# A two-layer decoder trunk on one core: a new opening with plain fp32 products, another PSUM bank for the compression, and layer 1's last sums in place

## The chip, the core and the metric

One core of a Trainium2 chip runs the kernel in one launch. Its engines are TensorE (PE, with its weight loads as PEld), VectorE (DVE), ScalarE (ACT), GpSimd (POOL) and SyncE (SP), which issues most of the transfers. The metric is the device time of one execution in microseconds, as the median of several runs; lower is better.

## What is computed

Two layers over a sequence of 1024 tokens and a width of 1024. The core of the reference, cut:

```python
def reference(x, c, positions, w_in, ..., w_up, w_down):
    cond = jax.nn.silu(c)
    for l in range(DEPTH):
        mod = cond @ w_mod[l] + b_mod[l]
        sh1, sc1, gt1, sh2, sc2, gt2 = [m[:, None, :] for m in jnp.split(mod, N_MOD, axis=-1)]
        h = rms_norm(x, norm_g[l, 0]) * (1.0 + sc1) + sh1
        y = mixer_block(h, positions, w_in[l], ..., w_o[l])
        x = x + gt1 * rms_norm(y, norm_g[l, 1])
        h = rms_norm(x, norm_g[l, 2]) * (1.0 + sc2) + sh2
        y = jnp.square(jax.nn.relu(h @ w_up[l])) @ w_down[l]
        x = x + gt2 * rms_norm(y, norm_g[l, 3])
    return x
```

`mixer_block` projects h with one matrix w_in and feeds four groups of 256 features: a gated convolution of width 3, a sparse attention (its keys and values compressed by blocks of 32 tokens with `cmp_w1`, `cmp_w2` and a position table `cmp_pos`, selected blocks, and a window), a gated linear attention, and a chunked gMLP. Each group's output is normalised, and the four go through one output projection w_o.

## The kernel before

Activations lie feature-major, in tiles of 128 features x 512 tokens; the sequence is two halves `hf` of T = 512 tokens, and eight tiles k = 0..7 make the width. A product is taken in three passes over fp32r tiles that are split into a high and a low part (`mm3`, L174 to L177): high by high, high by low, low by high. `gemm` (L179) does this for one output tile over eight k, and fetches the weights in units of four k: a transfer to `raw_a`, `raw_b` or `raw_f`, a cast on ACT (L167) and a subtraction on DVE (L131) give `w_a`, `w_b`, `w_f`. The letter is the lane, with buffers of its own.

The order of the program is `start()`, `mix(0,0)`, `mix(0,1)`, `ff(0,0)`, `mix(1,0)`, `ff(0,1)`, `mix(1,1)`, `ff(1,0)`, `ff(1,1)`, with layer and half as arguments. The order of the instructions on each engine is made from this by the scheduler of the language: an instruction stands the earlier the higher its rank, and `tc.high_priority(offset=-LATER[l, hf])` lowers the rank of a mixer's residual and of the norm behind it. Tiles of a named region may take the space of a region that was closed, tile by tile, as soon as its last reader is done. PSUM has eight banks, by tags: `mm` 2, `ff` 2, `s` 2, `t` 1, `pv` 1.

`start()` (L269) makes the rope tables (17 x 512 products, sent to DRAM as `cosd` and `sind`), the silu of the condition (`cond`, L293 to L296), the norm factor R of the first half (`rms_R`, L192 to L204: squares on ACT, sums on DVE, one product with a matrix of ones), and then for each k: two dots of a 512 KB slab of w_mod with cond (L243), the modulated tile h as a split pair (`make_h`, L207 to L213), and the six `EARLY` column blocks of w_in by `mm3`, from weights `w_k` that were split from `raw_k`: 8 x 6 x 3 = 144 products into six banks.

`mix(0,0)` runs gates, attention (`nsa_part`, with `compress()`, the scores L829 and L831, transposes L784 and weighted sums L789 and L790), and beside it, in lane b, the projections of the other groups (384 products `ps_mm<-h,w_b`), with two half dots per unit for the rest of the modulation (`mods_now`, L251). `compress()` has 32 products of tokens with `cmp_w1` (`ps_mm<-bp,kvt`, L717) and 32 of the position table (`ps_mm<-bp,p`, L717), sums of four partial results (L726, L737) and two small products (L747, L754), all in the `mm` banks. The output projection w_o follows (`ps_mm<-h,w_a`).

`ff_body` goes over eight groups of four hidden tiles: `up` makes hidden tiles by `gemm`, `down` adds a group's 8 x 12 products to the eight sums y. The last group's sums are written to new tiles `yf` of a region "fin", whose space is that of the mixer that ran beside, and `finish` normalises them and adds the residual, with tiles `xo` that come from DRAM. In the last body, `ff(1,1)`, the last group is done in place. The mixer's own residual (L957 to L963) does the same with tiles `yo`, and `make_h` gives h for the up-projection of the same half.

Of the kernel before, what the change touches and what calls it, by code (L numbers as in the profile page):

```python
# [9 lines left out]
I32 = mybir.dt.int32  # L10
# [8 lines left out]
LATER = {(0, 0): 0, (0, 1): 800, (1, 0): 800, (1, 1): 800}  # L19
# [16 lines left out]
def trunk_kernel(ctx, tc, xT, c, pos, freq, sel, w_in, conv_w, cmp_pos, cmp_w1, cmp_w2,  # L36
# [70 lines left out]
    def load_params(l, names):  # L107
        src = {"ng": norm_g, "bmod": b_mod, "conv": conv_w, "gain": gains}
        for n in names:
            dma(out=par[l][n], in_=src[n][l])  # L110
# [95 lines left out]

    def make_h(xt, R, Ac, shc, ks=range(8)):  # L207
        h = []
        for k in ks:
# [59 lines left out]
    def start():  # L269
        d = par[0]  # L270
        early = {}
        rope_tables()
        with region("kw", "right") as kw, region("su") as su:
            def mk(src, shape):
                t = su.tile(shape, F32, name="mw", tag="mw", bufs=4)
                dma(out=t, in_=src)
                return t

            def wload(n, kh):
                raw = kw.tile([128, 4, 128], F32, name="raw_k", tag="raw_k", bufs=6)  # L280
                dma(out=raw, in_=w_in[0, n, :, 4 * kh:4 * kh + 4, :])
                return raw

            def wsplit(raw):
                hi, lo = (kw.tile([128, 4, 128], F32R, name="w_k", tag="w_k", bufs=12) for _ in range(2))
                A.copy(hi, raw)
                sub(lo, raw, hi.bitcast(F32))
                return hi, lo

            for hf in range(2):  # L290
                t1, t2 = (su.tile([128, T], F32, name="ct", tag="ct", bufs=4) for _ in range(2))
                ch = cond[:, hf * T:hf * T + T]
                dma(out=ch, in_=c[:, hf * T:hf * T + T].to_broadcast([128, T]))  # L293
                logsig(t2, ch, t1)
                A.activation(t2, t2, AF.Exp)
                mul(ch, ch, t2)  # L296
            xt = load_x(0)
            load_params(0, ("ng", "bmod"))
            R = rms_R(xt, 1.0 / 1024)
            bm = d["bmod"].rearrange("p (j k) -> p j k", k=8)  # L300
            hs = []
            for k in range(8):
                ma = work.tile([128, 2, 1], F32, name="ma", tag="ma", bufs=4)
                for j in (0, 1):
                    mod_dot(0, j, k, mk, ma[:, j, :])
                add(d["mod"][:, 0:2, k:k + 1], ma, bm[:, 0:2, k:k + 1])
                mod_scale(0, 1, slice(k, k + 1))
                if k % 4 == 0:
                    raws = [wload(n, k // 4) for n in EARLY]
                hs += make_h(xt, R, d["A1"], d["mod"][:, 0, :], (k,))  # L310
                if k % 4 == 0:
                    ws = {n: wsplit(r) for n, r in zip(EARLY, raws)}
                for i, n in enumerate(EARLY):
                    if k == 0:
                        early[n] = ps(("mm", "mm", "ff", "ff", "s", "s")[i])
                    hi, lo = ws[n]
                    mm3(early[n], hi[:, k % 4, :], lo[:, k % 4, :], hs[k][0], hs[k][1], k == 0, k == 7)
        load_params(0, ("conv", "gain"))
        load_params(1, ("ng", "bmod", "conv", "gain"))
# [26 lines left out]
    def rope_tables():  # L346
        with region("rp") as rp:
# [3 lines left out]
            fr = rp.tile([128, 1, 8], F32, name="fr")  # L351
            dma(out=fr, in_=freq.unsqueeze(0).to_broadcast([128, 1, 8]))
            sl = rp.tile([17, 256], F32, name="sl")
            dma(out=sl, in_=sel)
            pi = rp.tile([128, 8, 1], I32, name="pi")
            dma(out=pi, in_=pos.unsqueeze(2))
# [22 lines left out]
            for hf in range(2):  # L379
# [5 lines left out]
                for w, dst in ((0, cosd), (128, sind)):  # L385
                    p = ps("s")
# [243 lines left out]
    def nsa_part(l, hf, h, rg, gates, early={}):  # L630
# [70 lines left out]

        def compress():
# [8 lines left out]
            def partial(col):  # L711

                hid = ps("mm", (128, 2, 128))
# [31 lines left out]
            kc = ps("mm", (128, 2, 64))  # L745
# [6 lines left out]
            vc = ps("mm", (128, 64))  # L752
# [225 lines left out]
    def ff_body(l, hf, step):  # L978
# [88 lines left out]

    h, early = start()
# [96 lines left out]
```

## Time and profile before

| | us |
|---|---|
| median of 3 runs (lowest, highest) | 2611.32 (2610.13, 2612.88) |
| the profiled execution | 2618.0 |
| its span, first to last instruction | 2616.3 |
| PE busy | 2488.0 (95% of the span) |
| DVE busy | 1631.3 (62%) |
| ACT busy | 1308.9 (50%) |
| mean granted clock of PE | 0.980 |

Times in the profile count from the first instruction of the span. A busy PE can run at a clock below its full one, so the windows give the granted clock beside the busy time. A plain product of two fp32 tiles appears as two records of one instruction, so "x2" is one product.

### The profile page before, as it was taken

How to read it: one execution, taken by the hardware profiler on the slowest of the kernel's cores; microseconds unless marked ns; L12 is line 12 of the kernel's file. 1: busy time of each engine (PE TensorE's matmuls, PEld its weight loads, DVE VectorE, ACT ScalarE, POOL GpSimd, SP SyncE). 2: the span in 40 equal slices, each digit the busy share in tenths (PEclk: the TensorE clock that was granted, in tenths of full speed). 3: DMA queues.
4: the chain of work that ended last, by engine and by line, in shares of the span. 5: the costliest groups of instructions: out<-in, count | busy, mean ns of one | idle time of the engine just before them, and what ended most of it. 6: DMA issues, size and time to landing. Idle time of an engine off the chain costs nothing.

```text
span 2616.3 us, 34392 instructions
## 1 busy us (share of the span) xinstructions
PE 2488.0 (95%) x11834; PEld 1985.6 (76%) x11834; DVE 1631.3 (62%) x3425; ACT 1308.9 (50%) x2657; POOL 53.9 (2%) x65
## 2 busy tenths in 40 slices
PE   5798899999999999999999999999999997999997
PEld 3666677777777878887787787877788875788886
DVE  7697675467887587445676476554577745634445
ACT  3465545445565456344365455444466744443433
POOL 0100000010000000000100000000100000000000
PEclk9898899999999999999999999999999999999999
DMA  8443233355434444223423354322422134333332
GB/s 280 141 151 94 91 122 121 110 152 153 127 117 142 153 157 146 93 78 105 146 77 92 94 157 141 103 81 77 121 74 69 61 107 150 127 98 97 97 97 75
DMA packets 176200, 305.79 MB, mean 117 GB/s; under 512 B 21573, under 2 KB 33434, under 8 KB 176026
## 3 DMA queue, kind: packets, MB, share of 16 engines
q1 hardware_dynamic: 176026, 303.60, 37.6%
q8 instruction: 93, 1.52, 0.2%
q14 instruction: 81, 0.66, 0.1%
HBM read 281.50 MB, written 17.83 MB: 114 GB/s over the span
## 4 chain that ended last, share of the span: by engine, by line
PE 83%; DVE 8%; DMA 5%; ACT 2%; issue 1%; SPq 0%; DVEq 0%; ACTq 0%
PE ps_ff L175 17%; PE ps_ff L176 17%; PE ps_ff L177 17%; PE ps_mm L176 7%; PE ps_mm L177 7%; PE ps_mm L175 7%; DMA raw_f<-in_w_mod_dram 2%; PE ps_mm L784 1%; DMA raw_b<-in_w_mod_dram 1%; PE ps_pv L790 1%; PE ps_pv L789 1%; PE ps_s L829 1%; PE ps_t L199 1%; PE ps_s L831 1%; PE ps_t L784 1%
## 5 line engine op out<-in xcount | busy, mean ns | idle before, releaser
L167 ACT CAST w_f<-raw_f 128x512 fp32r<-128x512 f32 x504 | 311.8, 619 | 430.5 <-PE ps_ff L176 409.0
L131 DVE TENSOR_TENSOR w_f<-raw_f,w_f 128x512 fp32r<-128x512 f32 x504 | 350.7, 697 | 177.7 <-ACT w_f L167 166.6
L175 PE MATMUL ps_ff<-hid,w_f 128*128 128x512 f32 x992 | 395.2, 399 | 21.4 <-DVE yf L137 12.7
L177 PE MATMUL ps_ff<-h,w_f 128*128 128x512 f32 x1024 | 405.4, 396 | 1.2 <-DVE w_f L131 1.2
L176 PE MATMUL ps_ff<-h,w_f 128*128 128x512 f32 x1024 | 402.7, 393 | 0.0
L175 PE MATMUL ps_ff<-h,w_f 128*128 128x512 f32 x1024 | 402.7, 393 | 0.0
L176 PE MATMUL ps_ff<-hid,w_f 128*128 128x512 f32 x992 | 392.1, 395 | 1.5 <-DVE hid L131 1.5
L177 PE MATMUL ps_ff<-hid,w_f 128*128 128x512 f32 x992 | 391.3, 394 | 0.0
L175 PE MATMUL ps_mm<-h,w_a 128*128 128x512 f32 x784 | 317.1, 405 | 6.2 <-ACT h L226 5.1
L177 PE MATMUL ps_mm<-h,w_a 128*128 128x512 f32 x784 | 315.7, 404 | 6.7 <-DVE w_a L131 6.7
L176 PE MATMUL ps_mm<-h,w_a 128*128 128x512 f32 x784 | 313.6, 401 | 1.2 <-DVE h L131 1.2
L167 ACT CAST w_a<-raw_a 128x512 fp32r<-128x512 f32 x196 | 121.3, 620 | 297.7 <-PE ps_mm L176 276.8
L131 DVE TENSOR_TENSOR w_a<-raw_a,w_a 128x512 fp32r<-128x512 f32 x196 | 135.0, 690 | 171.2 <-ACT w_a L167 167.3
L175 PEld LDWEIGHTS ps_ff<-hid,w_f 128*128 128x128 f32 x992 | 187.8, 189 | 69.7 <-DVE yf L137 15.2
L177 PEld LDWEIGHTS ps_ff<-h,w_f 128*128 128x128 f32 x1024 | 192.3, 188 | 45.8 <-issue 3.4
L175 PEld LDWEIGHTS ps_ff<-h,w_f 128*128 128x128 f32 x1024 | 192.4, 188 | 42.6 <-issue 3.1
L176 PEld LDWEIGHTS ps_ff<-h,w_f 128*128 128x128 f32 x1024 | 192.4, 188 | 42.0 <-issue 2.2
L176 PEld LDWEIGHTS ps_ff<-hid,w_f 128*128 128x128 f32 x992 | 187.9, 189 | 44.4 <-issue 2.9
L177 PEld LDWEIGHTS ps_ff<-hid,w_f 128*128 128x128 f32 x992 | 187.8, 189 | 41.2 <-issue 1.4
L137 DVE TENSOR_TENSOR y<-y,ps_ff 128x512 f32<-128x512 f32 (+1 forms) x208 | 138.0, 664 | 123.7 <-PE ps_ff L177 122.4
L175 PEld LDWEIGHTS ps_mm<-h,w_a 128*128 128x128 f32 x784 | 149.3, 190 | 45.8 <-ACT h L226 6.7
L177 PEld LDWEIGHTS ps_mm<-h,w_a 128*128 128x128 f32 x784 | 149.0, 190 | 44.9 <-DVE w_a L131 8.6
(390 smaller groups left out, 3618.3 us busy)
## 6 DMA issues: line engine op xcount, KB each, us to landing
raw_f<-in_w_up_dram SPq DMA_DIRECT2D x256, 256.0 KB, 2.7
raw_f<-in_w_down_dram SPq DMA_DIRECT2D x256, 256.0 KB, 2.7
raw_a<-in_w_in_dram SPq DMA_DIRECT2D x132, 256.0 KB, 2.7
raw_f<-in_w_mod_dram SPq DMA_DIRECT2D x112, 256.0 KB, 2.8
raw_a<-in_w_o_dram SPq DMA_DIRECT2D x64, 256.0 KB, 2.7
raw_b<-in_w_mod_dram SPq DMA_DIRECT2D x48, 256.0 KB, 2.9
mw<-in_w_mod_dram SPq DMA_DIRECT2D x16, 512.0 KB, 5.1
bp<-in_cmp_w_dram SPq DMA_DIRECT2D x32, 256.0 KB, 5.3
```

The lines of the kernel that those rows point to most:

```text
L131: V.tensor_tensor(out=out, in0=a, in1=b, op=ALU.subtract)
L137: eng.tensor_tensor(out=out, in0=a, in1=b, op=ALU.add)
L167: A.copy(hi, raw)
L175: PE.matmul(ps_ap, wh, xh, start=start, stop=False)
L176: PE.matmul(ps_ap, wh, xl, start=False, stop=False)
L177: PE.matmul(ps_ap, wl, xh, start=False, stop=stop)
L199: PE.matmul(p, ones, acc, start=True, stop=True)
L784: PE.transpose(tp[0:kn, hh, :], cols(h0 + hh), ident)
L789: PE.matmul(pv[:, h0:h0 + nh, :], vst, th[0:kn], start=first[0], stop=False)
L790: PE.matmul(pv[:, h0:h0 + nh, :], vst, tl[0:kn], start=False, stop=last)
L829: PE.matmul(sp[:, 0:w], qh[:, h0 + hh, :], KX[:, 128 * k0:128 * k0 + w], start=True, stop=False)
L831: PE.matmul(sp[:, 0:w], ql[:, h0 + hh, :], KX[:, 128 * k0:128 * k0 + w], start=False, stop=True)
```

## The change

1. `start()` is written anew. The condition's transfers and the first two slabs of w_mod are issued first, then x, the six first halves of the early weights (`raw_k`, 4 of 8 k), slabs for k = 1 and 2, and the six late halves (`w_r`). The slabs have 6 buffers for 4. The eight squares go to PE one by one, as plain fp32 products with ones that accumulate. For k < 4 each early block has one plain fp32 product, raw weights by the unsplit tile t; for k >= 4 the weights are split (`w_k`) and go through `mm3` as before. The tile is made by a product with R in place on DVE and a scale with bias on ACT, and then split for the later users. Parameters and rope inputs are issued on POOL's queue, and the rope tables stand behind the loop in the program, with the bank `pv`.
2. `compress()` of `mix(0,0)` uses the bank `pv`, that of the other mixers `mm` as before; the position part stands ahead of the token part. The tiles of lane b are opened ahead of `start()`.
3. In `ff_body` for layer 1, the last group's sums stay in y, and `xo` comes from the tiles of h; `LATER[(1, 1)]` is 6000 where it was 800.

The diff, cut to its core:

```diff
-LATER = {(0, 0): 0, (0, 1): 800, (1, 0): 800, (1, 1): 800}
+LATER11 = 6000
+LATER = {(0, 0): 0, (0, 1): 800, (1, 0): 800, (1, 1): LATER11}
...
     def start():
         d = par[0]
         early = {}
-        rope_tables()
-        with region("kw", "right") as kw, region("su") as su:
+        with region("kw", "right") as kw, region("rp") as rp, region("su") as su:
             def mk(src, shape):
-                t = su.tile(shape, F32, name="mw", tag="mw", bufs=4)
+                t = su.tile(shape, F32, name="mw", tag="mw", bufs=6)
                 dma(out=t, in_=src)
                 return t
-            def wload(n, kh):
+            def wload(n):
                 raw = kw.tile([128, 4, 128], F32, name="raw_k", tag="raw_k", bufs=6)
-                dma(out=raw, in_=w_in[0, n, :, 4 * kh:4 * kh + 4, :])
+                dma(out=raw, in_=w_in[0, n, :, 0:4, :])
                 return raw
+            def wlate(n):
+                raw = hp.tile([128, 4, 128], F32, name="w_r", tag="h", bufs=32)
+                dma(out=raw, in_=w_in[0, n, :, 4:8, :])
+                return raw
+
...
+            def mload(k):
+                return [mk(w_mod[0, 8 * j + k], [128, 1024]) for j in (0, 1)]
+
+            halves = [slice(hf * T, hf * T + T) for hf in range(2)]
+            for c_ in halves:
+                dma(out=cond[:, c_], in_=c[:, c_].to_broadcast([128, T]))
+            load_params(0, ("ng", "bmod"), P.dma_start)
+            small = rope_loads(rp)
+            mws = {0: mload(0)}
+            xt = load_x(0)
+            raws = [wload(n) for n in EARLY]
+            mws[1] = mload(1)
+            mws[2] = mload(2)
+            late = [wlate(n) for n in EARLY]
+            for c_ in halves:
                 t1, t2 = (su.tile([128, T], F32, name="ct", tag="ct", bufs=4) for _ in range(2))
-                ch = cond[:, hf * T:hf * T + T]
-                dma(out=ch, in_=c[:, hf * T:hf * T + T].to_broadcast([128, T]))
-                logsig(t2, ch, t1)
+                logsig(t2, cond[:, c_], t1)
                 A.activation(t2, t2, AF.Exp)
-                mul(ch, ch, t2)
-            xt = load_x(0)
-            load_params(0, ("ng", "bmod"))
-            R = rms_R(xt, 1.0 / 1024)
+                mul(cond[:, c_], cond[:, c_], t2)
+            p = ps("t")
+            for k in range(8):
+                sq = nt()
+                A.activation(sq, xt[k], AF.Square)
+                PE.matmul(p, ones, sq, start=k == 0, stop=k == 7)
+            R = rstd(p, 1.0 / 1024, su.tile([128, T], F32, name="R0"))
             bm = d["bmod"].rearrange("p (j k) -> p j k", k=8)
             hs = []
             for k in range(8):
                 ma = work.tile([128, 2, 1], F32, name="ma", tag="ma", bufs=4)
-                for j in (0, 1):
-                    mod_dot(0, j, k, mk, ma[:, j, :])
+                for j, raw in enumerate(mws.pop(k)):
+                    V.tensor_tensor_reduce(out=raw, in0=raw, in1=cond, scale=1.0, scalar=0.0,
+                                           op0=ALU.mult, op1=ALU.add, accum_out=ma[:, j, :])
                 add(d["mod"][:, 0:2, k:k + 1], ma, bm[:, 0:2, k:k + 1])
                 mod_scale(0, 1, slice(k, k + 1))
-                if k % 4 == 0:
-                    raws = [wload(n, k // 4) for n in EARLY]
-                hs += make_h(xt, R, d["A1"], d["mod"][:, 0, :], (k,))
-                if k % 4 == 0:
-                    ws = {n: wsplit(r) for n, r in zip(EARLY, raws)}
+                if k + 3 < 8:
+                    mws[k + 3] = mload(k + 3)
+                mul(xt[k], xt[k], R)
+                t = su.tile([128, T], F32, name="ct", tag="ct", bufs=4)
+                A.activation(t, xt[k], AF.Identity, scale=d["A1"][:, k:k + 1], bias=d["mod"][:, 0, k:k + 1])
+                hs.append(split(t))
                 for i, n in enumerate(EARLY):
                     if k == 0:
                         early[n] = ps(("mm", "mm", "ff", "ff", "s", "s")[i])
-                    hi, lo = ws[n]
-                    mm3(early[n], hi[:, k % 4, :], lo[:, k % 4, :], hs[k][0], hs[k][1], k == 0, k == 7)
-        load_params(0, ("conv", "gain"))
-        load_params(1, ("ng", "bmod", "conv", "gain"))
+                    if k < 4:
+                        PE.matmul(early[n], raws[i][:, k, :], t, start=k == 0, stop=False)
+                    else:
+                        hi, lo = late[i]
+                        mm3(early[n], hi[:, k - 4, :], lo[:, k - 4, :], hs[k][0], hs[k][1], False, k == 7)
+                if k == 1:
+                    late = [wsplit(r) for r in late]
+            rope_tables(rp, *small)
+        load_params(0, ("conv", "gain"), P.dma_start)
+        load_params(1, ("ng", "bmod", "conv", "gain"), P.dma_start)
         return hs, early
     def mods_now(l, js, lane):
...
+        CT = "pv" if (l, hf) == (0, 0) else "mm"
+
...
-                hid = ps("mm", (128, 2, 128))
+                hid = ps(CT, (128, 2, 128))

...
-            hx = partial(lambda jj, i: k5[:, jj, i // 8:i // 8 + 32, 2 * (i % 8)])
-            hp_ = ps("mm", (128, 2, 32))
-            for jj in range(2):
-                PE.matmul(hp_[:, jj, :], hx[:, jj, :], sel4, start=True, stop=True)
...
                 hb = partial(lambda jj, i: pos2[:, jj, 2 * i:2 * i + 32])
-                pb = ps("mm", (128, 2, 2))
+                pb = ps(CT, (128, 2, 2))
                 for jj in range(2):
                     PE.matmul(pb[:, jj, :], hb[:, jj, :], sel4[:, 0:2], start=True, stop=True)
                 A.copy(posb[l], pb[:, :, 0:1])
+            hx = partial(lambda jj, i: k5[:, jj, i // 8:i // 8 + 32, 2 * (i % 8)])
+            hp_ = ps(CT, (128, 2, 32))
+            for jj in range(2):
+                PE.matmul(hp_[:, jj, :], hx[:, jj, :], sel4, start=True, stop=True)
...
-                with region("wb", "right") as lane_pool["b"]:
+                with wbs:

...
-            down(NGRP - 1, yo=lambda: rg.tile([128, T], F32, name="yf", tag="yf", bufs=8))
+            down(NGRP - 1, yo=None if l else lambda: rg.tile([128, T], F32, name="yf", tag="yf", bufs=8))
             R = rms_R(y, 1.0 / 1024)
             finish(slice(0, T), R,
-                   lambda k: load(rg.tile([128, T], F32, name="xo", tag="xo", bufs=4), xa[l][hf][:, k, :]),
+                   lambda k: load(rg.tile([128, T], F32, name="xo", tag="xo", bufs=4) if l == 0 else spare(),
+                                  xa[l][hf][:, k, :]),
                    xb[hf] if l + 1 < DEPTH else out[hf])
             return norm(l + 1, hf, y) if l + 1 < DEPTH else None
...
+    wbs = ExitStack()
+    lane_pool["b"] = wbs.enter_context(region("wb", "right"))

```

PE, right behind the opening's products (`ps_s<-h,w_k` is the last of them; `bp` is a quarter of cmp_w, `kvt` the compressed keys' and values' tokens, `w2g` the gate weights), before:

```order
L177 MATMUL ps_s<-h,w_k 128x512
L717 MATMUL ps_mm<-bp,kvt 32x128 x32
L507 MATMUL ps_ff<-w2g,lrT 128x128 x3
L486 MATMUL ps_t<-ident,nt 128x64 x4
L507 MATMUL ps_ff<-w2g,lrT 128x128
L690 MATMUL ps_t<-ident,p 128x128 x4
L512 MATMUL ps_ff<-tri,g 128x128 x4
L726 MATMUL ps_mm<-sel_124,p 128x32 x2
L717 MATMUL ps_mm<-bp,p 32x128 x32
```

PE at the same place in the changed kernel (there `mm3` is L176 to L178, and the compression's products L750):

```order
L178 MATMUL ps_s<-h,w_k 128x512
L517 MATMUL ps_t<-ident,nt 128x64 x4
L176 MATMUL ps_mm<-h,w_b 128x512
L177 MATMUL ps_mm<-h,w_b 128x512
L178 MATMUL ps_mm<-h,w_b 128x512
```

Behind the early products stand products of lane b, where the compression and the gates stood: 72 of them ahead of the first score, 84 ahead of the compression's `ps_pv<-bp,kvt`, and 139 ahead of the first weighted sum, for 12 to 15 before.

PE at the end of attention in mix(0,0) and the start of the output projection (`ps_mm<-h,w_a`), before, where the last weighted sum (`ps_pv<-w_a,VC`) stands 82 products of lane b ahead of this piece:

```order
L176 MATMUL ps_mm<-h,w_b 128x512
L177 MATMUL ps_mm<-h,w_b 128x512
L199 MATMUL ps_ff<-nt,ones 128x512
L199 MATMUL ps_t<-nt,ones 128x512
L175 MATMUL ps_mm<-h,w_a 128x512
L176 MATMUL ps_mm<-h,w_a 128x512
```

In the changed kernel:

```order
L822 MATMUL ps_pv<-w_a,VW 128x512
L823 MATMUL ps_pv<-w_a,VW 128x512
L817 MATMUL ps_t<-ident,p 32x128 x4
L822 MATMUL ps_pv<-w_a,VC 128x512
L823 MATMUL ps_pv<-w_a,VC 128x512
L200 MATMUL ps_t<-nt,ones 128x512
L176 MATMUL ps_mm<-h,w_a 128x512
L177 MATMUL ps_mm<-h,w_a 128x512
```

The last product of lane b now stands ahead of the last seven weighted sums, and the norm product of attention (`ps_t<-nt,ones`) directly behind the last of them.

DVE around the last sums of ff(1,0) (`yo` is the mixer's output with its residual, `A_112` and `mod_109` scale and shift of its norm, `y<-y,ps_ff` or `yf<-y,ps_ff` a last sum), before:

```order
L140 SCALAR_TENSOR_TENSOR nt<-yo,A_112,nt 128x512 x2
L140 SCALAR_TENSOR_TENSOR h<-nt,mod_109,h 128x512 x2
L140 SCALAR_TENSOR_TENSOR nt<-yo,A_112,nt 128x512 x2
L137 TENSOR_TENSOR yf<-y,ps_ff 128x512 x2
L140 SCALAR_TENSOR_TENSOR h<-nt,mod_109,h 128x512 x2
L137 TENSOR_TENSOR nt<-nt 128x512
L137 TENSOR_TENSOR yf<-y,ps_ff 128x512
L131 TENSOR_TENSOR w_f<-raw_f,w_f 128x512
```

In the changed kernel:

```order
L132 TENSOR_TENSOR w_f<-raw_f,w_f 128x512
L138 TENSOR_TENSOR y<-y,ps_ff 128x512
L132 TENSOR_TENSOR w_f<-raw_f,w_f 128x512
L138 TENSOR_TENSOR y<-y,ps_ff 128x512
L132 TENSOR_TENSOR w_f<-raw_f,w_f 128x512
L141 SCALAR_TENSOR_TENSOR nt<-yo,A_112,nt 128x512 x2
L141 SCALAR_TENSOR_TENSOR h<-nt,mod_109,h 128x512 x2
```

All eight last sums stand ahead of `make_h`, where only two stood within it and six behind it; the residual's scalings and adds (`yo<-yo,G`, `yo<-yo,xo`) stand among the first of these sums.

## Rows read from the trace of the kernel before

**Rows 1.** Page, busy us of the engines (share of the span) xinstructions.

```profile
PE 2488.0 (95%) x11834; PEld 1985.6 (76%) x11834; DVE 1631.3 (62%) x3425; ACT 1308.9 (50%) x2657; POOL 53.9 (2%) x65
```

**Rows 2.** Windows: length, busy us per engine, PE clock, DMA share, GB/s.

```profile
20.00:30.00 10.00, 3.20 (x4) 0.50 (x2) 6.28 (x10) 8.48 (x17) 0.00 (x0) 1.00 1.00 350
30.00:40.00 10.00, 0.00 (x0) 0.00 (x0) 8.84 (x19) 0.60 (x3) 0.00 (x0) 1.00 0.87 310
40.00:50.00 10.00, 9.24 (x31) 7.07 (x32) 10.00 (x22) 2.15 (x3) 0.00 (x0) 1.00 1.00 356
...
75.65:112.40 36.75, 20.69 (x204) 17.73 (x204) 28.02 (x85) 15.21 (x50) 7.66 (x6) 0.67 0.42 122
112.40:256.70 144.30, 131.02 (x689) 97.34 (x687) 116.70 (x345) 83.16 (x207) 5.41 (x8) 0.95 0.40 122
```

**Rows 3.** Timeline of PE: start us, us, instruction, count, [idle before <-releaser].

```profile
40.75 1.22 PE L175 MATMUL ps_mm<-h,w_k 128*128 128x512 f32 x2 [11.93 <-ACT h L213]
...
75.43 0.39 PE L177 MATMUL ps_s<-h,w_k 128*128 128x512 f32 x1
...
112.95 0.39 PE L789 MATMUL ps_pv<-w_a,VS 128*128 128x512 f32 x1
```

**Rows 4.** Timeline of DVE, opening and the stage behind it.

```profile
30.82 1.22 DVE L243 CUSTOM_DVE_ANT_0 mw<-mw,cond 128x1024 f32<-128x1024 f32 x1
...
81.87 0.69 DVE L131 TENSOR_TENSOR w_b<-raw_b,w_b 128x512 fp32r<-128x512 f32 x1
...
87.67 0.66 DVE L131 TENSOR_TENSOR w_b<-raw_b,w_b 128x512 fp32r<-128x512 f32 x1
```

**Rows 5.** Timeline of PE, a product of two plain fp32 tiles.

```profile
2214.14 2.08 PE L199 MATMUL ps_t<-nt,ones 128*128 128x512 f32 x2 [5.56 <-DVE nt L137]
```

**Rows 6.** Chain of waits, such a product at another time: start us, us.

```profile
2190.86 0.86 PE ps_t L199 x2
```

**Rows 7.** Waits of PE, 20 to 110 us: total us, times, longest.

```profile
PE ps_mm L717 <- DMA p<-in_cmp_pos_dram: 6.1, 1, 6.1
...
PE ps_t L690 <- DVE gates L140: 5.4, 1, 5.4
PE ps_mm L747 <- DVE p L134: 3.5, 1, 3.5
```

**Rows 8.** Lines of DVE by form, 76 to 260 us: busy us, mean ns.

```profile
L251 DVE CUSTOM_DVE_ANT_0 raw_b<-raw_b,cond 128x512 f32<-128x512 f32 x48 | 35.6, 745 | 18.4 <-DMA raw_b<-in_w_mod_dram 18.2
L131 DVE TENSOR_TENSOR w_b<-raw_b,w_b 128x512 fp32r<-128x512 f32 x28 | 19.2, 685 | 5.6 <-ACT w_b L167 5.5
```

**Rows 9.** Timeline of PE, attention's end and w_o, layer 0.

```profile
256.25 0.49 PE L790 MATMUL ps_pv<-w_a,VC 32*128 32x512 f32 x1
...
290.56 0.79 PE L176 MATMUL ps_mm<-h,w_a 128*128 128x512 f32 x1 [1.16 <-DVE h L131]
```

**Rows 10.** Waits of PE, 1265 to 1300 us, compression of layer 1.

```profile
PE ps_mm L717 <- DMA bp<-in_cmp_w_dram: 3.5, 5, 1.1
```

**Rows 11.** Timeline of PE, last sums of ff(1,0).

```profile
2200.64 0.39 PE L175 MATMUL ps_ff<-hid,w_f 128*128 128x512 f32 x1
...
2228.31 0.79 PE L175 MATMUL ps_ff<-hid,w_f 128*128 128x512 f32 x1 [12.09 <-DVE yf L137]
...
2246.67 0.39 PE L177 MATMUL ps_ff<-hid,w_f 128*128 128x512 f32 x1
2246.90 0.39 PE L175 MATMUL ps_ff<-h,w_f 128*128 128x512 f32 x1
```

**Rows 12.** Timeline of DVE, the same place.

```profile
2193.72 5.38 DVE L140 SCALAR_TENSOR_TENSOR yo<-yo,G,nt 128x512 f32<-128x512 f32 x8
...
2217.64 1.42 DVE L140 SCALAR_TENSOR_TENSOR nt<-yo,A,nt 128x512 f32<-128x512 f32 x2 [3.55 <-ACT nt L204]
...
2228.77 1.41 DVE L140 SCALAR_TENSOR_TENSOR h<-nt,mod,h 128x512 fp32r<-128x512 f32 x2
```

**Rows 13.** Chain of waits, the same place.

```profile
2203.15 6.22 DMA xo<-xb
```

More of the change, by code (lines that the diff above doesn't have):

```diff
@@ L105, in trunk_kernel, with load_params @@
         par.append(d)
-    def load_params(l, names):
+    def load_params(l, names, load=dma):
         src = {"ng": norm_g, "bmod": b_mod, "conv": conv_w, "gain": gains}
         for n in names:
-            dma(out=par[l][n], in_=src[n][l])
+            load(out=par[l][n], in_=src[n][l])
     KS = const.tile([128, 1024], F32R, name="KS")
@@ L205, in rstd, with make_h @@
         return R
-    def make_h(xt, R, Ac, shc, ks=range(8)):
+    def make_h(xt, R, Ac, shc):
         h = []
-        for k in ks:
+        for k in range(8):
             t = nt()
@@ L271, in start @@
         early = {}
-        rope_tables()
-        with region("kw", "right") as kw, region("su") as su:
+        with region("kw", "right") as kw, region("rp") as rp, region("su") as su:
             def mk(src, shape):
-                t = su.tile(shape, F32, name="mw", tag="mw", bufs=4)
+                t = su.tile(shape, F32, name="mw", tag="mw", bufs=6)
                 dma(out=t, in_=src)
                 return t
-            def wload(n, kh):
+            def wload(n):
                 raw = kw.tile([128, 4, 128], F32, name="raw_k", tag="raw_k", bufs=6)
-                dma(out=raw, in_=w_in[0, n, :, 4 * kh:4 * kh + 4, :])
+                dma(out=raw, in_=w_in[0, n, :, 0:4, :])
[3 more added lines that the diff above has]
+                dma(out=raw, in_=w_in[0, n, :, 4:8, :])
                 return raw
             def wsplit(raw):
-                hi, lo = (kw.tile([128, 4, 128], F32R, name="w_k", tag="w_k", bufs=12) for _ in range(2))
+                hi, lo = (hp.tile([128, 4, 128], F32R, name="w_k", tag="h", bufs=32) for _ in range(2))
                 A.copy(hi, raw)
@@ L288, in wsplit @@
                 return hi, lo
-            for hf in range(2):
+            def mload(k):
[12 more added lines that the diff above has]
+            for c_ in halves:
                 t1, t2 = (su.tile([128, T], F32, name="ct", tag="ct", bufs=4) for _ in range(2))
-                ch = cond[:, hf * T:hf * T + T]
-                dma(out=ch, in_=c[:, hf * T:hf * T + T].to_broadcast([128, T]))
-                logsig(t2, ch, t1)
+                logsig(t2, cond[:, c_], t1)
                 A.activation(t2, t2, AF.Exp)
-                mul(ch, ch, t2)
-            xt = load_x(0)
-            load_params(0, ("ng", "bmod"))
-            R = rms_R(xt, 1.0 / 1024)
+                mul(cond[:, c_], cond[:, c_], t2)
+            p = ps("t")
+            for k in range(8):
+                sq = nt()
+                A.activation(sq, xt[k], AF.Square)
+                PE.matmul(p, ones, sq, start=k == 0, stop=k == 7)
+            R = rstd(p, 1.0 / 1024, su.tile([128, T], F32, name="R0"))
             bm = d["bmod"].rearrange("p (j k) -> p j k", k=8)
@@ L344, in trunk_kernel, with rope_loads, rope_tables @@
     sind = dram.tile([2, 128, T], F32, name="sind")
-    def rope_tables():
-        with region("rp") as rp:
+    def rope_loads(rp):
+        fr = rp.tile([128, 1, 8], F32, name="fr")
+        P.dma_start(out=fr, in_=freq.unsqueeze(0).to_broadcast([128, 1, 8]))
+        sl = rp.tile([17, 256], F32, name="sl")
+        P.dma_start(out=sl, in_=sel)
+        pi = rp.tile([128, 8, 1], I32, name="pi")
+        P.dma_start(out=pi, in_=pos.unsqueeze(2))
+        return fr, sl, pi
+    def rope_tables(rp, fr, sl, pi):
+        if True:
             def tk(n):
                 return rp.tile([128, 8, 8], F32, name=n)
[L351 to L356, printed above, removed]
             pf = rp.tile([128, 8, 1], F32, name="pf")
@@ L385, in rope_tables @@
                 for w, dst in ((0, cosd), (128, sind)):
-                    p = ps("s")
+                    p = ps("pv")
                     PE.matmul(p, sl[:, w:w + 128], st, start=True, stop=True)
@@ L744, in compress @@
             mul(hs, hs, act)
-            kc = ps("mm", (128, 2, 64))
+            kc = ps(CT, (128, 2, 64))
             for r in range(2):
@@ L751, in compress @@
                 A.copy(KC[rs, r, 32 * hf:32 * hf + 32], kc[rs, 0, 0:32])
-            vc = ps("mm", (128, 64))
+            vc = ps(CT, (128, 64))
             hr = slice(32 * hf, 32 * hf + 32)
```

## The prediction

> **What bounds the kernel now.** I read the page first, to see that PE is busy for 95% of the span [rows 1]: a gain can only come from the few stretches where PE waits or runs at its lower clock, so the next views were the windows and PE's waits of those stretches, and then the timelines there, which say what each wait ends with. There are four places.
>
> The *opening*: PE does nothing of the layer until 40.75 us, then runs its 144 early products without a gap to 75.65 [rows 3]. The reader should see that DVE starts on the modulation only at 30.82 [rows 4], because the silu of the condition is queued behind weight casts, while the transfers run at 310 to 356 GB/s [rows 2]. The *stage behind it*: up to the first weighted sum of attention at 112.95 [rows 3] PE is busy 20.69 of 36.75 us at a clock of 0.67, between the two levels of 1.2 and 2.4 GHz [rows 2]. Three waits of 6.1, 5.4 and 3.5 us make up most of the idle time [rows 7]; DVE is busy 28.02 us of it. The *end of attention*: its last weighted sum is at 256.25, but the output projection runs steadily only from 290.56 [rows 9]. *ff(1,0)*: the last sums begin at 2200.64 and the next up-projection at 2246.90 [rows 11], 46.3 us. Products start 0.23 us apart there [rows 11], so the 96 last sums are 96 x 0.23 = 22.1 us and the rest, 24.2, is waiting, a norm product and the lower clock. Its longest wait, 12.09 us, is for the sum into a new yf tile.
>
> **The opening, removed and added.** In place of 144 products there are 24 plain and 72 split ones. A plain fp32 product takes 0.86 us at the full clock [rows 6] and 2.08 behind an idle stretch [rows 5]; three products of a split take 3 x 0.23 = 0.69. The 24 plain ones thus cost 24 x (0.86 - 0.69) = 4.1 us more on PE at the full clock, and 33 more at the lower one; the eight squares that go to PE take 6.9. What is bought is the start: condition and first slabs are issued first, and the first product needs no split. Ahead of it lie 5.0 MB (condition 0.5, two slabs 1, x 2, six raw halves 1.5), 14.3 us at 350 GB/s [rows 2]; with 9 us for the start of the queue and the chain of norm and scaling behind it (an estimate), it comes at 23 instead of 40.75. Its end is set by the transfers: by the order of SP's queue 17.6 MB lie ahead of the last slab's landing, 50 us at 350 and 57 at 310 GB/s, and with 5 us of start I take 58. Behind it come dot, scaling, split, about 4 us, and the eighteen products of that k, 18 x 0.23 = 4.1: 66 us against 75.65. PE's own chain would allow 23 + 24 x 0.86 + 72 x 0.23 = 60. With every plain product at 2.08 it ends at 89. So the opening gives 9.7, at best 15.7, at worst it loses 13.7. The six fewer splits take work off DVE and ACT beside it; the small loads on POOL's queue and the rope tables behind the loop lie under those transfers and cost nothing; if they were late, the first rotation would wait for the tables.
>
> **A rule against the plain product.** The rows give 0.86 against 0.69. The Trainium skill, FP8 and Floating Point Precision, section TensorE Precision Notes, says that true FP32 takes four passes through the array. By four passes of 0.23 the 24 products would cost 5.5 us more on PE instead of 4.1, and the trace nearly agrees (0.86 is 3.7 passes). The sum goes by the rows.
>
> **The compression's bank and the earlier lane.** With its own bank "pv" and with the lane's tiles opened ahead, PE's order has 139 lane-b products before the first weighted sum, where it had 15, and none behind the last, where it had 82. One unit of 12 products is 12 x 0.23 = 2.8 us of PE, and of DVE a split and two dots, 0.685 + 2 x 0.745 = 2.2 us [rows 8]. PE's idle time there is thus filled, and what is late next is DVE: 28.0 us, less the two units of before with their stretched ops (some 6), plus 12 x 2.2 = 26, is 48 us, at 92% busy 52. From 63, when DVE is free of the opening, the first weighted sum comes at 115: 2 us *later* than before. From there to the last one it took 143.3 us with 287 lane products between; now there are 245, 3.5 units fewer, and as DVE and PE are both nearly full there (116.70 and 131.02 of 144.30 [rows 2]) I take 3.5 x 2.2 = 8 us off, and put 5 on, since the last seven weighted sums have no products between them and PE waits for each. The end: the norm product of attention now follows its last weighted sum at once, where 82 lane products (18.9 us) and another group's norm stood ahead. I take 12 us for norm, scaling and split (norm 1.4 behind the product [rows 5, 12], scaling and split at about 0.7 each for two tiles, the product at 0.9 to 2.1), where it was 290.56 - 256.25 = 34.3: 22 less. Up to the output projection: 2 - 8 + 5 - 22 = 23 us gained, the opening's 9.7 included in the 2. Bounds: if DVE is no limit, the first sum comes at 66 + 139 x 0.23 + 8 = 106 and 32 are gained; if the lane's units and the bare end cost what they save, nothing.
>
> **The compression of layer 1**: its position part now goes ahead of the rest and the products that wait for cmp_w come 36 later. The 3.5 us of waits [rows 10] go; I take 3 (0 to 3.5).
>
> **Last sums of ff(1,0).** In place, they no longer wait for the tiles of the mixer, and with the residual ranked later the order is: seven products, the norm product, the rest. The norm product ends at about 2202.3 (0.9 behind seven products), its scale is there 1.4 later, at 2203.7. DVE then does 8 scalings, 5.4 us [rows 12], and two adds, 2210.5, before the first sum at 2211.2 frees a bank. PE has run two outputs by 2206.3, so it *still waits* about 5 us. After that DVE has 6 adds, 7 sums, 8 weight splits and 7 squares' adds, 28 x 0.69 = 19.3 [rows 8], and PE's six outputs (16.6) go along with it: 2230.5. Then norm product and scale, 2.3: the first tile of h at 2233.5, the others 1.4 apart (2217.64 to 2230.18 for eight, two sums among them [rows 12]), so the first up-projection ends at about 2244.7. Before it ended at 2246.90 + 24 x 0.23 = 2252.4. Gain 7.7 us; a third of the stall, not all of it, since make_h now comes *behind* the sums and nothing covers it. Best, with the first bank free at once, 14; worst, if the residual's loads of 6.22 us [rows 13] stand twice in DVE's queue, it loses 5.
>
> **Sum**: 23 + 3 + 7.7 = 33.7 us, against the profiled execution's 2618.0 (2616.3 span and 1.7 around it) 2584.3. The median is 6.7 below that execution, so on its scale 2611.3 - 33.7 = **2577.6 us**.
>
> **Rivals.**
> *The lane in front of attention paces it.* PE works in order: whatever stands behind twelve units waits for them, and a unit waits for its slab, cast, split and dots. The two splits of before were 5.8 us apart [rows 4]. At p us a unit, the first weighted sum is at 74 + 12p, and the total change is (74 + 12p - 113) - 25 - 10.7. At 5.8 that is -5, at 7.2 it is +11: slower, from p = 6.7 on. Against it: in those 5.8 us DVE did other work as well, and transfers were under half of their peak. 2622.
> *The clock stays low in the opening.* PE idles until the first transfers, and a plain product behind an idle stretch took 2.08 [rows 5]. The opening ends at 89, 23 us behind the forecast, and the stage with it: 33.7 - 23 = 11 us gained, 2600.6. The Trainium skill, TensorE: Matmul & The Clock Gate, section HAM oscillation — how this bites in real kernels, warns of just this loop, bursts of products between waits for transfers. Against it: from 40 to 50 us, right behind 11.93 us of idle, the granted clock reads 1.00 [rows 2].
> *The bare end gives the gain back.* Seven weighted sums, each with a transpose, copy and split behind the other, at 5 us rather than 3 each, and the gap at 20 instead of 12: 22 less gained, 2600.
> *The last sums still wait.* The residual's adds hold the sums up in DVE's queue and part 2 gives nothing: 2585, and 2590 at its worst.
> *PE is never short of units*, DVE's extra is hidden: 32 + 3 + 10 = 45 gained, 2566.
>
> **Chances.** The forecast within 8 us either way, or the last sums without a gain beside it, 0.52. More than that, as far as 2558, 0.15. The bare end or the low clock, 2586 to 2604, 0.22. No change within 0.2% (5.2 us, about what a measurement of this kernel can tell) 0.04; the lane's pace, slower, 0.07. Faster by over 0.2% is thus 0.89. For 8 in 10 the range takes in most of the second and third, 2559 to 2601.
>
> **What the profile would show.** First early product near 23 us and last near 66, with 0.86 us for a plain one; lane-b products right behind it and no wait above 4 us up to the first weighted sum at 110 to 116; the output projection within 15 us of the last weighted sum; no wait for cmp_w near 1270; a wait of some 5 us two outputs into the last sums, none of 12, and then h arriving every 1.4 us. The forecast is wrong if the early products end behind 75, if the first weighted sum is behind 125, or if a gap above 20 us stays ahead of the output projection.

## The result, and the profile after

The changed kernel took 2586.59 us (median of 4 runs, 2582.14 to 2588.90) against 2612.10 for the kernel before in the same set, 25.5 us gained. The ratio is 0.9889, 95% interval 0.9874 to 0.9904, by which it would be 29 us; it is not the quotient of the two medians, which is 0.9902. In a second set it was 2585.32 against 2615.77, ratio 0.9881 (0.9866 to 0.9896), 30.5 us. The prediction was 2577.6 in a range of 2559 to 2601: the sign, the order of size and the range held, and the point lies 9 us too low, a little more than the 8 us either way that it gave the best chance.

Windows of the changed kernel, columns as in [rows 2]; the last three go from the last early product to the first weighted sum, to the last one, and to the output projection:

```profile
20.00:30.00 10.00, 8.46 (x24) 3.41 (x24) 8.69 (x14) 4.33 (x8) 0.00 (x0) 1.00 1.04 397
30.00:40.00 10.00, 8.81 (x12) 3.21 (x13) 9.86 (x27) 8.79 (x16) 0.00 (x0) 0.66 1.04 401
40.00:50.00 10.00, 10.00 (x25) 4.50 (x24) 9.34 (x21) 3.11 (x6) 0.00 (x0) 1.00 1.03 401
68.50:122.50 54.00, 50.23 (x414) 40.09 (x414) 43.77 (x126) 27.25 (x72) 8.28 (x6) 0.97 0.54 166
122.50:262.60 140.10, 124.10 (x559) 88.55 (x557) 108.54 (x309) 78.24 (x197) 5.19 (x8) 0.91 0.32 101
262.60:274.00 11.40, 3.38 (x5) 1.07 (x4) 5.39 (x10) 6.47 (x12) 0.64 (x1) 0.50 0.27 81
```

PE, idle from 30 to 40 us in [rows 2], now works there, at a granted clock of 0.66, and the stage behind the opening runs at 0.97, not 0.67. The same places in the timeline of PE, which answer to [rows 3, 9]:

```profile
23.48 1.88 PE L339 MATMUL ps_mm<-ct,raw_k 128*128 128x512 f32 x4
...
28.72 1.12 PE L418 MATMUL ps_pv<-nt,sl 17*128 17x512 f32 x2
30.52 1.12 PE L418 MATMUL ps_pv<-nt,sl 17*128 17x512 f32 x2 [0.68 <-ACT of L420]
32.31 2.07 PE L418 MATMUL ps_pv<-nt,sl 17*128 17x512 f32 x2 [0.67 <-ACT of L420]
34.31 3.78 PE L339 MATMUL ps_mm<-ct,raw_k 128*128 128x512 f32 x4
...
64.30 0.62 PE L176 MATMUL ps_mm<-h,w_k 128*128 128x512 f32 x2
...
68.16 0.39 PE L178 MATMUL ps_s<-h,w_k 128*128 128x512 f32 x1
...
122.52 0.40 PE L822 MATMUL ps_pv<-w_a,VS 128*128 128x512 f32 x1
...
262.61 0.79 PE L823 MATMUL ps_pv<-w_a,VC 32*128 32x512 f32 x1
267.56 2.05 PE L200 MATMUL ps_t<-nt,ones 128*128 128x512 f32 x2 [4.17 <-DVE nt L138]
273.46 0.80 PE L176 MATMUL ps_mm<-h,w_a 128*128 128x512 f32 x1 [3.85 <-ACT h L227]
```

The first early product came at 23.48 (23 was forecast) and the last at 68.16 (66); four records are two plain products here, 1.88 us at the full clock and 3.78 at the lower. The `ps_pv<-nt,sl` are products of the rope tables, and at 64.30 the eighteen products of the last k begin. The lane-b products made attention *later*, 122.52 for 112.95, and the output projection earlier, 273.46 for 290.56 (288.61 if its first product is counted in the kernel before too). PE's waits around the last sums of ff(1,0), which answer to [rows 11]:

```profile
PE ps_ff L176 <- DVE y L138: 5.9, 2, 4.8
PE ps_ff L176 <- ACT h L214: 3.0, 1, 3.0
PE ps_ff L176 <- ACT r L1023: 1.6, 2, 1.0
PE ps_ff L177 <- DVE hid L132: 1.1, 1, 1.1
```

To see where the gain lies, this table compares, run by run, when PE had started as many products of lane a and of the feed-forward (`ps_mm<-h,w_a`, `ps_ff<-h,w_f`, `ps_ff<-hid,w_f`) as the kernel before had at five marks of its trace (us earlier than there):

| traced execution | 400 | 1225 | 1500 | 2150 | 2550 |
|---|---|---|---|---|---|
| changed kernel | 17.8 | 18.6 | 27.7 | 28.5 | 36.1 |
| the same, second set (rep_after) | 18.4 | 20.8 | 30.4 | 27.3 | 35.1 |
| kernel before, once more (rep_before) | -0.9 | -0.2 | 1.2 | 1.4 | 1.8 |
| open_only | 6.7 | 9.4 | 8.8 | 7.9 | 8.1 |
| open_cmp | 8.2 | 9.9 | 18.7 | 17.7 | 17.4 |
| no_bank | 10.8 | 13.9 | 21.3 | 19.4 | 29.9 |
| no_wb | 12.8 | 15.5 | 22.7 | 23.5 | 31.4 |
| no_last | 14.9 | 16.1 | 25.9 | 23.9 | 24.1 |
| inplace_only | 16.1 | 14.9 | 22.6 | 23.2 | 36.4 |
| later_only | 13.1 | 12.3 | 20.0 | 19.3 | 10.8 |
| wo_order | 18.3 | 19.4 | 28.3 | 28.5 | 36.4 |

Up to 400 us lie opening and first attention, between 1225 and 1500 the compression of layer 1, between 2150 and 2550 the last sums. The two traced executions of the changed kernel (2582.1 and 2581.9) are the shortest of their sets and the traced one of before, 2618.0, is 6 us above its median, so 36 us between traces is 25 to 31 between medians. Differences of a few us between single rows of the table are thus no finding by themselves.

### The profile page after: what moved, and what is told of

Same layout as the page of the kernel before. It is cut to its first block, busy times and chain, and to the rows that moved or that the text cites. A ratio compares the mean times of both kernels' runs of the same rounds, so it can differ in the third digit from the quotient of the medians.

```text
span 2580.4 us, 34356 instructions
## 1 busy us (share of the span) xinstructions
PE 2491.9 (97%) x11824; PEld 1977.9 (77%) x11824; DVE 1618.9 (63%) x3412; ACT 1312.8 (51%) x2659; POOL 59.2 (2%) x76
## 5 line engine op out<-in xcount | busy, mean ns | idle before, releaser
L176 PE MATMUL ps_ff<-h,w_f 128*128 128x512 f32 x1024 | 403.2, 394 | 6.7 <-ACT h L214 3.0
L176 PE MATMUL ps_ff<-hid,w_f 128*128 128x512 f32 x992 | 393.6, 397 | 13.3 <-DVE y L138 10.2
L178 PE MATMUL ps_ff<-h,w_f 128*128 128x512 f32 x1024 | 405.2, 396 | 0.8 <-DVE w_f L132 0.8
L178 PE MATMUL ps_ff<-hid,w_f 128*128 128x512 f32 x992 | 389.9, 393 | 0.0
L176 PE MATMUL ps_mm<-h,w_a 128*128 128x512 f32 x784 | 316.4, 404 | 5.3 <-ACT h L227 3.9
L178 PE MATMUL ps_mm<-h,w_a 128*128 128x512 f32 x784 | 314.9, 403 | 5.5 <-DVE w_a L132 5.5
L176 PEld LDWEIGHTS ps_ff<-hid,w_f 128*128 128x128 f32 x992 | 187.1, 189 | 59.8 <-DVE y L138 9.4
L176 PEld LDWEIGHTS ps_ff<-h,w_f 128*128 128x128 f32 x1024 | 192.5, 188 | 51.1 <-ACT h L214 3.8
L178 PEld LDWEIGHTS ps_ff<-h,w_f 128*128 128x128 f32 x1024 | 192.7, 188 | 45.5 <-issue 3.6
L178 PEld LDWEIGHTS ps_ff<-hid,w_f 128*128 128x128 f32 x992 | 187.0, 188 | 41.0 <-issue 1.4
L138 DVE TENSOR_TENSOR y<-y,ps_ff 128x512 f32<-128x512 f32 (+1 forms) x216 | 143.3, 664 | 114.3 <-PE ps_ff L178 112.8
L176 PEld LDWEIGHTS ps_mm<-h,w_a 128*128 128x128 f32 x784 | 148.6, 189 | 45.0 <-ACT h L227 5.4
L178 PEld LDWEIGHTS ps_mm<-h,w_a 128*128 128x128 f32 x784 | 148.6, 190 | 43.5 <-DVE w_a L132 7.1
```

The source lines that it names most:

```text
L138: eng.tensor_tensor(out=out, in0=a, in1=b, op=ALU.add)
L176: PE.matmul(ps_ap, wh, xh, start=start, stop=False)
L178: PE.matmul(ps_ap, wl, xh, start=False, stop=stop)
```

## The experiments

### Both kernels once more

**rep_after.** No edit. 

> The changed kernel once more. Theory S (the change's gain is that of the traces: opening and stage about 17, compression of layer 1 about 10, last sums about 7): if the two profiled executions, 36 us apart, are typical, the medians of this set stand 36 us apart, and the new profile has the same marks (last early product at 68, first steady output projection at 274). Theory V (single executions of either kernel wander by several us, the profiled one of before was a long one and that of after a short one): the medians stand about 25 us apart again, and in this profile one stage that no part of the change touches, or the compression of layer 1, differs by 4 us or more from the first profile of the same kernel.

Measured: 2585.32 (2581.85 to 2590.82) against 2615.77, gain 30.5. The marks from the first early product to the output projection were the same within 0.9 us. **rep_before.** No edit. 

> The kernel before once more, ratio 1.000 within 0.002. Theory V: in this profile the compression of layer 1 near 1270 us costs PE a different amount (between 3 and 10 us of idle and low clock) than in the first, as its transfers happen to fall. Theory S: it loses the same 10 us there.

Measured: ratio 1.0006 (0.9997 to 1.0016); its trace loses the same time at the compression, within 1.4 us. So the compression is no chance of one execution, against theory V; but V is right that executions of the changed kernel wander, and five traced executions with PE's products in one order up to layer 1's last sums show where: changed kernel, rep_after, no_last, inplace_only and later_only are 13.1 to 18.4 us ahead at 400. The early products of the one furthest behind, the run later_only, in the timeline of PE:

```profile
25.11 3.62 PE L339 MATMUL ps_mm<-ct,raw_k 128*128 128x512 f32 x4
...
37.97 3.78 PE L339 MATMUL ps_mm<-ct,raw_k 128*128 128x512 f32 x4
...
72.42 0.39 PE L178 MATMUL ps_s<-h,w_k 128*128 128x512 f32 x1
```

Its first two plain products took 3.62 us, where the changed kernel's took 1.88, and the opening ended at 72.42, 4.3 later: the granted clock from 20 to 30 us is 0.66 here and 1.00 in the other four.

### The opening alone

**open_only.** All of the change but `start()` undone:

```diff
-        CT = "pv" if (l, hf) == (0, 0) else "mm"
+        CT = "mm"
...
-LATER11 = 6000
+LATER11 = 800
```

> The new opening alone: bank mm, lane b opened in the mixer, compression in the old order, last sums and rank as before. Theory O (the opening's seven us are handed on): early products end at 68 as in the changed kernel, everything behind is 7 us earlier, ratio 0.997 (2605). Theory L (the lane cannot use the earlier start, and DVE paces the stage): the seven us are lost again before the output projection, ratio 1.000. Theory W (the freed tiles alone change the order behind the opening as well): more than 12 us gained, 0.995 or less.

Measured: 2609.66, ratio 0.9973 (0.9963 to 0.9984), 6 to 7 us. Theory O: the opening's 6.5 us (68.94 for 75.43) are handed on whole, 6.7 at the mark of 400.

### Bank, early tiles, and the compression's order

**no_bank.**

```diff
-        CT = "pv" if (l, hf) == (0, 0) else "mm"
+        CT = "mm"
```

> The changed kernel with the compression of mix(0,0) back in the mm banks; all else stays. PE's order then has 82 lane products behind the last weighted sum again, as before. Theory B (the bank is what lets the lane go ahead, and that is worth some 10 us of the 16 to 17 at the start of mix(0,1)): 8 to 12 us slower than the changed kernel, ratio to the kernel before 0.992, and the output projection starts 34 us behind the last weighted sum again. Rival (the stage is paced by DVE, and where the lane's products stand does not matter): within 3 us of the changed kernel.

Measured: 2588.70, ratio 0.9888 (0.9871 to 0.9905). Its timeline of PE:

```profile
98.06 0.80 PE L822 MATMUL ps_pv<-w_a,VS 128*128 128x512 f32 x1 [1.15 <-ACT w_a L819]
...
246.84 0.49 PE L823 MATMUL ps_pv<-w_a,VC 32*128 32x512 f32 x1
...
265.75 0.39 PE L178 MATMUL ps_mm<-h,w_b 128*128 128x512 f32 x1
...
279.20 0.79 PE L176 MATMUL ps_mm<-h,w_a 128*128 128x512 f32 x1 [5.09 <-ACT h L227]
```

The gap of 32 us ahead of the output projection is back, as theory B said, but the price is not: attention starts and ends 24 and 16 us earlier without the lane ahead of it. Of the 8 to 12 us expected, the trace shows 5.7 at the output projection. The ratio lies 0.0007, 2 us, above that of the second set and level with the first (0.9889), well inside the intervals: whether the bank brings anything is not settled, and 8 us or more would lie at the intervals' far ends.

**no_wb.**

```diff
-    wbs = ExitStack()
-    lane_pool["b"] = wbs.enter_context(region("wb", "right"))
...
-                with wbs:
+                with region("wb", "right") as lane_pool["b"]:
```

> The changed kernel with lane b's tiles opened in the mixer, as before, and the bank as in the changed kernel. PE's order has 142 lane products ahead of the first weighted sum, for 139. Theory B: the early tiles are not what counts, within 3 us of the changed kernel. Rival (the early fetch of the lane's first weights is what keeps PE busy behind the opening): PE waits at the first lane products for their weights, some 5 us slower.

Measured: 2584.30, ratio 0.9872 (0.9855 to 0.9890): no difference, theory B here.

**open_cmp.** The run open_only, with the position part ahead of the token part. 

> The new opening and the compression's order, position part first, without the bank, the early tiles and the change of the last sums. It differs from the run of the new opening alone (ratio 0.9973) only by that order. Theory C (the order takes away waits for transfers and the low clock behind them in layer 1's compression near 1270 us, 9 to 10 us in the traces, not the 3 of my sum): ratio 0.9937, 9 us under that run. Rival (only the waits of 3.5 us go, the rest of the 9 comes from other parts of the change): 0.996.

Measured: 2600.10, ratio 0.9938 (0.9925 to 0.9952), 0.0035 or 9 us under open_only. The table has it between 1225 and 1500: 8.8 us, where open_only has none. The windows of the kernel before, same columns, show why it is more than the waits of [rows 10]:

```profile
1270.00:1280.00 10.00, 6.71 (x62) 3.89 (x62) 5.69 (x13) 0.60 (x1) 3.80 (x3) 0.86 0.87 281
1280.00:1290.00 10.00, 9.23 (x46) 6.76 (x43) 5.12 (x11) 2.23 (x4) 0.00 (x0) 0.63 0.25 50
1290.00:1300.00 10.00, 10.00 (x107) 8.34 (x105) 4.12 (x18) 4.50 (x12) 0.00 (x0) 1.00 0.52 158
```

Behind the idle pieces the granted clock was 0.86 and 0.63, so PE was "busy" for 9.23 of 10 us at little over half its pace. What the two clocks lack to 1.00 is 1.4 and 3.7 us; with the waits of 3.5 that makes 8.6. The same window in open_only and then in open_cmp, which differ by this order alone:

```profile
1265.00:1275.00 10.00, 6.33 (x69) 3.31 (x70) 1.29 (x4) 0.37 (x1) 1.87 (x2) 0.68 0.63 197
```

```profile
1265.00:1275.00 10.00, 8.93 (x96) 7.24 (x96) 8.63 (x20) 2.68 (x6) 1.38 (x2) 1.00 0.77 232
```

In the changed kernel the three windows of that place, 1250 to 1280 us, read 1.00 as well.

### The last sums

**no_last.** 

> The changed kernel with layer 1's last sums in new tiles and the residual at its old rank. Theory S: 7 us slower than the changed kernel, PE waits 12 us for the first sum again near 2190. Rival (the waits move elsewhere and the last sums do not matter): within 2 us.

Measured: 2594.07 (2593.52 to 2594.90), ratio 0.9913 (0.9899 to 0.9927), 6 to 8 us slower by the ratios; the wait of 12.1 us is back. **inplace_only.**

```diff
-LATER11 = 6000
+LATER11 = 800
```

> The changed kernel with the last sums in place and the residual of mix(1,1) at its old rank of 800. Theory I (the new tiles' wait for make_h was the stall, in place removes it, and the rank only adds): the wait of 12 us goes, PE still waits about 5 us, and the time is within 3 us of the changed kernel. Rival (at the old rank DVE runs the whole residual and make_h ahead of the sums, so that PE waits for banks just the same): 7 us slower, like the run without both.

Measured: 2580.87 (2579.27 to 2584.85), ratio 0.9858 (0.9845 to 0.9872), 6 to 8 us *faster* than the changed kernel by the ratios; the interval overlaps a little with that of the second set and not with that of the first. Neither theory expected it. **later_only.**

```diff
-            down(NGRP - 1, yo=None if l else lambda: rg.tile([128, T], F32, name="yf", tag="yf", bufs=8))
+            down(NGRP - 1, yo=lambda: rg.tile([128, T], F32, name="yf", tag="yf", bufs=8))
```

> The changed kernel with the residual of mix(1,1) ranked at 6000 and the last sums in new tiles. The tiles take the mixer's space, which is free only when make_h has read it; ranked later, the residual stands still further behind. Theory I: the wait stays or grows, 7 to 12 us slower than the changed kernel, PE waits 12 us or more for the first new tile. Rival (the rank alone moves the sums ahead): within 3 us of the changed kernel.

Measured: 2604.67, ratio 0.9946 (0.9933 to 0.9958), 15 to 17 us slower than the changed kernel by the ratios, more than either theory. PE's longest waits around the last sums, in inplace_only and then in later_only:

```profile
PE ps_ff L176 <- DVE y L138: 2.3, 1, 2.3
PE ps_ff L177 <- DVE hid L132: 2.0, 3, 1.3
PE ps_ff L176 <- ACT r L1023: 1.0, 1, 1.0
```

```profile
PE ps_t L200 <- DVE nt L138: 17.1, 1, 17.1
PE ps_ff L176 <- DVE yf L138: 12.1, 1, 12.1
```

In place is worth 13.2 us in its trace (23.2 to 36.4), the pair 7.6 (28.5 to 36.1; 7.8 in rep_after), and neither 0.2 (no_last): the later rank *costs* 5 to 6. The ratios agree, 14 us between no_last and inplace_only. With the sums in place the residual runs beside them at the old rank, and the wait for h (`ACT h`, 3.0 in the changed kernel) is not among the waits of inplace_only. Alone, the rank puts the residual so late that PE waits 29 us.

### The plain products

**mm3_open.** On no_wb, each of the first four k by `mm3`, its weights split in pairs of k:

```diff
-                    if k < 4:
-                        PE.matmul(early[n], raws[i][:, k, :], t, start=k == 0, stop=False)
+                    hi, lo = first[i] if k < 4 else late[i]
```

> The changed kernel with lane b opened in the mixer (the run no_wb is its neighbour, 2584) and all 48 early products of the opening's first four k as split ones, their weights split on ACT and DVE in pairs of k. Theory P (the plain product's own price is small, since what it saves is the split in front of the first product): PE needs 24 x 0.17 = 4 us less, the first product comes some 4 us later behind six more casts, and the time is within 3 us of that neighbour. Rival (the opening is now limited by PE from 23 to 68 us, so that the cheaper products come through): early products end at 65 or before and 3 to 4 us are gained. Second rival (the splits crowd ACT and DVE ahead of the slabs' dots): 4 us or more lost.

Measured: 2584.61, ratio 0.9873 (0.9858 to 0.9888), against 0.9872 for no_wb; first early product at 25.50, last at 69.14. Theory P: plain or split makes no difference that the medians can tell. The two traces do not compare, since PE was at its lower clock at 25 us in the one of no_wb, whose opening ended at 72.43.

### Two further edits

**wo_order.** The changed kernel with

```diff
-                gemm(p, "a", w_o[l, o], outs, (6, 7, 4, 5, 2, 3, 0, 1) if opening else range(8))
+                gemm(p, "a", w_o[l, o], outs)
```

> The changed kernel with the output projection of mix(0,0) going over its eight inputs in the order 0 to 7 rather than attention first. In the changed kernel PE idles or runs at its lower clock for 11 us between the last weighted sum and the first product of the output projection, since attention's norm stands in front of it, though the other six inputs are ready. Theory: 18 products fill that gap, and the gap's idle time of 8.0 us shrinks to 3 or less: 4 to 8 us faster than the changed kernel. Rival: PSUM has two mm banks, so only two outputs can begin, DVE's splits of their weights come late, and the gain is under 2 us.

Measured: 2580.21 (2580.09 to 2580.51), ratio 0.9860 (0.9846 to 0.9873), 5 us under the changed kernel's median. Its timeline of PE:

```profile
267.93 0.80 PE L176 MATMUL ps_mm<-h,w_a 128*128 128x512 f32 x1
...
269.08 0.79 PE L823 MATMUL ps_pv<-w_a,VC 32*128 32x512 f32 x1
```

The output projection now begins ahead of the last weighted sum. At 400 us the trace is 18.3 ahead, though its opening ended at 70.93, 2.8 later than the changed kernel's. With the intervals overlapping a little, the gain over the changed kernel is likely, not certain.

**wo_rope.** That, and the rope tables held back until the modulation of k = 2 is there. 

> The changed kernel with the output projection in the order 0 to 7 (2580.2 in its own run) and the rope tables held back until the modulation of k = 2 is there, so that their products stand behind the early ones. In the changed kernel PE spends 28.7 to 34.3 us on three of them and their waits, and then runs four early products at the lower clock. Theory R (PE is the limit of the opening): the early products end at 62 to 64 rather than 68 to 71, and 3 to 5 us are gained over 2580.2. Rival (the slabs' landing, or attention's DVE work behind, is the limit): early products end earlier but the first weighted sum does not, within 2 us of 2580.2, or slower, as the first rotation waits for its tables.

Measured: 2591.10, ratio 0.9894 (0.9881 to 0.9908), 9 us slower than wo_order by the ratios. Its timeline of PE:

```profile
23.28 3.78 PE L339 MATMUL ps_mm<-ct,raw_k 128*128 128x512 f32 x4 [3.01 <-ACT ct L333]
...
51.09 0.73 PE L176 MATMUL ps_mm<-h,w_k 128*128 128x512 f32 x2 [2.43 <-ACT h L227]
...
68.48 0.39 PE L178 MATMUL ps_s<-h,w_k 128*128 128x512 f32 x1
...
81.80 1.12 PE L420 MATMUL ps_pv<-nt,sl 17*128 17x512 f32 x2
...
111.43 0.33 PE L864 MATMUL ps_s<-KS,qh 128*128 128x128 f32 x1
...
149.65 0.40 PE L824 MATMUL ps_pv<-w_a,VS 128*128 128x512 f32 x1
```

The rope tables no longer interrupt the early products, but the first ones ran at the lower clock (3.78), and the later ones wait for h at 51; they end at 68.48, 2.4 before wo_order and level with the changed kernel. Theory R, 62 to 64, falls. The tables' last product now stands at 81.80; the first score, which needs the rotated keys, comes at 111.43 (96.02 in wo_order), and with 168 lane products ahead of it, not 139, the first weighted sum is 23 us late. So the run is slower, as the rival said; that the late tables alone cause it is likely, not shown.

The compression's order was tried on the old banks only (open_cmp); wo_order and inplace_only in one kernel were not tried.

## Why the prediction was right, and where it missed

**The opening**: 6.4 us on the mean of five executions (3.0 to 7.7) for 9.7. Step that missed: "its end is set by the transfers". They ran at 397 to 401 GB/s, not the 310 to 350 I took. The last h was split on DVE by 58.9 us, and PE came to its products only at 64.30:

```profile
58.25 0.69 DVE L132 TENSOR_TENSOR h<-ct,h 128x512 fp32r<-128x512 f32 x1 [1.54 <-ACT h L227]
```

PE set the end, busy without a wait from 34 us on. My chain for it, 60, lacked three products of the rope tables with their waits (28.7 to 34.3, 5.6 us) and some 2 us of lower clock behind them: 68. What the end would be without them is not shown, since in wo_rope a lower clock and waits for h took their place. The price of a plain product was right (0.86), and mm3_open shows no difference from a split one.

Against the rival of the clock I misread a row. The window from 40 to 50 us of the kernel before reads 1.00, but its first products did not run at that pace:

```profile
43.69 0.80 PE L176 MATMUL ps_mm<-h,w_k 128*128 128x512 f32 x1
44.28 0.63 PE L177 MATMUL ps_mm<-h,w_k 128*128 128x512 f32 x1
```

They stand 0.42 to 0.64 us apart up to 44.7 and 0.23 from 45 on. So an idle stretch did cost pace there, and the rival deserved more weight.

**The stage behind it**: 16.1 us on the mean of those five executions at the mark of 400, opening included, for 23. Step that missed: "what is late next is DVE", first weighted sum at 115. It came at 122.5 (at 125.4 and 128.5 in two of the five, behind the 125 that I had named as a sign of being wrong), and DVE was busy 43.77 of 54.0 us, PE 50.23. PE was next: 139 lane products at 0.23 are 32.0, and the other 18.2 are gates, compression and scores, for which I had 8 in the bound. From there on the terms held: 140.1 us to the last weighted sum (140.3 forecast) and 10.9 to the output projection (12). That no part of the bank's own could be measured is the rival of no_bank, "where the lane's products stand does not matter", in another form, with PE and not DVE as the pace: work moved ahead of attention delays attention by itself.

**The compression of layer 1**: 7 to 10 us in the traces with the new order, 9 in the ratios, for 3 with 3.5 as the most. The mechanism was right and the term mis-sized: I counted the waits and not the lower clock that follows them, 5.1 us.

**The last sums**: 7.6 for 7.7, with the wait of 4.8 where 5 was forecast and h behind the sums as described. What I did not see is that the two edits pull apart: in place alone is 13.2, near my upper bound of 14, and the rank takes 5 to 6 back.

Two misses of 7 and 6 us in opposite directions left the sum of the traces (36) near the forecast (33.7): that the sum came so near is luck, though each part has the sign that was forecast. The medians gained less, 25.5 and 30.5 us, as the traced executions of the changed kernel were short ones and that of the kernel before a long one. The bare end did not come (10.9 us, not 20). The clock rival, at 2600.6, did not come in full, but part of it is there: a granted clock of 0.66 from 30 to 40 us, and in later_only from 20 to 30 as well.

## What to carry to other kernels

A wait of a few us on PE costs the wait and what follows at the lower clock: read the granted clock of the windows behind it, and the spacing of the products, before pricing its removal, here 9 us for 3.5. Moving filler work into a gap ahead of a serial chain delays the chain, here by 24 us for 32 us of filler; what is gained is only the idle and slow part of the gap, so price both ends. When two edits come together at one stall, take them one at a time: in place was worth 13 us, the rank beside it cost 5 to 6.

## What the hardware showed beyond expectation

The same instructions at 25 us ran at either clock in different executions: two plain products took 1.88 us in four of five traces and 3.62 in the fifth (2.88 in wo_order, whose products are the same up to the end of attention), and the opening ended between 67.7 and 72.4. The transfers of the opening reached 401 GB/s with slabs and raw halves back to back, where the windows of the kernel before showed at most 356 [rows 2].
